# Feature norms in a layer step: the mean by a constant matrix, 1/rms on 352 columns

## The chip, the cores and the metric

The kernel runs on one core of a Trainium2 chip. The metric is the device time of one execution in microseconds (us). A core has five engines that run side by side, each through its own instructions in their order: TensorE (PE in the profile; PEld is its weight load), VectorE (DVE), ScalarE (ACT), GpSimd (POOL) and SyncE (SP). TensorE writes to PSUM, a small memory of banks; VectorE and ScalarE read from it, and GpSimd does not in this kernel. Transfers between memory and the core are started from the queues of SP, POOL and ACT.

## The reference

One encoder layer for 2048 prompt tokens and 64 sample tokens, 1024 features each, in float32. Cut to what matters:

```python
def rms_norm(x, g):
    return x * lax.rsqrt(jnp.mean(x * x, axis=-1, keepdims=True) + EPS) * g

h = rms_norm(x, g_pre)
proj = h @ w_in                       # ten parts: vA, bA, cA, zA, q, f, iv, zB, gA, gB
yA = (silu(zA) * bA * causal_conv3(cA * vA, conv_w)) @ w_a_out
S_new, o = hgrn2_scan(S0, qq, kk, vv, logf)           # eight heads, chunks of 64 tokens
yB = (norm_per_head(o) * g_onorm * silu(zB)) @ w_b_out
out = (sigmoid(gA) * yA + sigmoid(gB) * yB) @ w_o
x = x + rms_norm(out, g_post)                         # first feature norm
gate = sigmoid(rms_norm(x, g_ple) @ w_ple_gate)       # second feature norm
x = x + (p @ w_ple_proj) * gate
```

## The kernel before

**Layout and blocks.** Features lie on the 128 partitions (eight tiles of 128 for 1024 features), tokens along the free axis. The 2112 tokens are cut into three blocks of 704, numbered 0 to 2, and each block into two halves of 352. A matrix product is written as three: the high part of the weights times the high part of the data, high times low, and low times high, each as a matmul on 352 columns in the type float32r. High parts are casts on ACT, low parts subtractions on DVE (`split`, line 184; for weights lines 214 and 184). Large products over weight pairs run as groups of seven smaller ones (`sgroup`, lines 357 to 359, and `in_turn`, lines 490 to 492); plain ones run through `mm3` (lines 523 to 525).

**Order of the work.** Every engine's order is fixed when the program is built. PE's is the leading one: after each product a hook (`hook`) may emit one step of a side job, and `placed` sets that step's matmuls behind the product just issued. Side jobs are Python generators: each `next` emits the work up to the next `yield`.

**The norms.** At the end of a block `final_norm` works as such a side job: first norm, scaling (line 1162), adding of x (1163), squares for the second norm (lines 629, 632, 633), second norm, scaling (1176) and split. In blocks 0 and 1 it runs on both halves together, among the gate groups of the next block, and `spread_out` gives its steps to the hooks in the pattern (0, 1, 0, 1), then (0, 1, 0) eight times, and so on. In block 2 there are two such jobs, one for each half: the first begins among the last products with `w_o` and the second runs in the gate products at the end. The ordering set of `behind_all` puts a step behind the copies and adds that the running products need.

**Inside a norm.** `acc` holds, for each token column, the squares summed over the eight feature tiles, still spread over 128 partitions. `col_rstd` (line 614) takes 128 columns of `acc` at a time as weights and multiplies them with a column of ones: the sum over partitions comes out with tokens on partitions, three columns for 352 tokens. `rstd_of` (line 585 on DVE, line 587 on POOL) computes (mean + EPS) to the power -0.5 on these three columns. `spread` (line 598) multiplies each column, repeated 128 times as weights, with the identity: each token's value stands again in all 128 partitions. Line 624 copies that from PSUM. `rms` does the first part in its first step and the spread and copy in its second.

**Who else calls these.** `rstd_of` also serves the norms of the attention heads (four columns or one) and the rows of x (one column, or six at the start). `spread` also serves the rows of x: at the start, and in `spread_all` for blocks 1 and 2.

**Queues and buffers.** Weights come in on SP's queue. POOL's queue fetches x for the residual (line 1153), spills gates and x (lines 738 and 1172), fetches them back (1043) and writes the output (1197). 52 ring buffers of 708 columns hold most tiles, five PSUM banks the products (`pg`) and three the small ones (`pa`).

Of the kernel before, what the change touches and what calls it, by code (L numbers as in the profile page):

```python
# [10 lines left out]
F32 = mybir.dt.float32  # L11
F32R = mybir.dt.float32r
I32 = mybir.dt.int32
AF = mybir.ActivationFunctionType
ALU = mybir.AluOpType
# [3 lines left out]
P = 128  # L19
D = 1024  # L20
# [62 lines left out]
def hybrid_step(  # L83
# [17 lines left out]
    V, A, G, T, SP = nc.vector, nc.scalar, nc.gpsimd, nc.tensor, nc.sync  # L101
# [3 lines left out]
    const = ctx.enter_context(tc.tile_pool(name="const", bufs=1))  # L105
# [9 lines left out]
    def nm(s):  # L115
        uid[0] += 1
        return f"{s}_{uid[0]}"

    def rt(n=BN, dt=F32):
        t = ring.tile([P, BN + 4], dt, tag="r", name=nm("r"))  # L120
        return t if n is None else t[:, :n]
# [4 lines left out]
    def ps_attn():  # L126
        return psa.tile([P, 512], F32, tag="pa", name=nm("pa"))
# [4 lines left out]
    def spill(kind, j):  # L132
        return dram.tile([P, BN], F32, tag=f"{kind}{j}", name=nm(kind), bufs=2)


    ident = const.tile([P, P], F32, tag="ident", name="ident")
    make_identity(nc, ident)
    ones = const.tile([P, 1], F32, tag="ones", name="ones")
    V.memset(ones, 1.0)
    mhalf = const.tile([P, 1], F32, tag="mhalf", name="mhalf")  # L140
    V.memset(mhalf, -0.5)
    vec = const.tile([P, 9, KB], F32, tag="vec", name="vec")
# [40 lines left out]
    def split(src, hi, lo):  # L183
        return A.copy(hi, src).ins, V.tensor_tensor(lo, src, hi.bitcast(F32), ALU.subtract).ins  # L184
# [49 lines left out]
    last, hooks, copies, adds = [None], [], [None], [None]  # L234

    def placed():

        return tc.issue_after(last[0]) if last[0] is not None else nullcontext()
# [288 lines left out]
    def cols_of(s):  # L527
        return slice(s["off"], s["off"] + s["n"])
# [51 lines left out]
    def tiles_of(n):  # L580

        return [(i, min(i * P, n - P)) for i in range((n + P - 1) // P)]

    def rstd_of(ms_ap, out_ap, scale, start=0):
        scaled = V.tensor_scalar(out_ap, ms_ap, scale, EPS, ALU.mult, ALU.add).ins
        shape = [out_ap.shape[0], out_ap.shape[1]]
        G.tensor_tensor(out_ap, out_ap, mhalf[start : start + shape[0], :].to_broadcast(shape), ALU.pow)
        return scaled

    def cols_tile(n):  # L590
        return small.tile([P, (n + P - 1) // P], F32, tag=f"cols{n}", name=nm("cols"))

    def spread(cols, n):

        pb = ps_attn()
        with placed():
            for i, o in tiles_of(n):
                T.matmul(pb[:, o : o + P], cols[:, i : i + 1].to_broadcast([P, P]), ident, start=True, stop=True)
        return pb[:, :n]

    def spread_all(cols):

        rs = rt()
        for h in range(2):
            A.copy(half(rs, h), spread(cols[h], HN))
        return rs

    def col_rstd(acc, n):

        pc = ps_attn()  # L610
        cols = cols_tile(n)
        with placed():
            for i, o in tiles_of(n):
                T.matmul(pc[:, i : i + 1], acc[:, o : o + P], ones, start=True, stop=True)
        rstd_of(pc[:, : cols.shape[1]], cols, 1.0 / D)
        return cols

    def rms(acc, out, segs, copy=A.copy):


        cols = [col_rstd(acc[:, cols_of(sg)], sg["n"]) for sg in segs]
        yield
        for sg, col in zip(segs, cols):
            copy(out[:, cols_of(sg)], spread(col, sg["n"]))
        yield

    def sum_squares(j, src, acc, n):
        if j == 0:
            A.activation(acc, src, AF.Square)
        else:  # L630
            sq = rt(n)
            A.activation(sq, src, AF.Square)
            V.tensor_tensor(acc, acc, sq, ALU.add)
# [507 lines left out]
    def final_norm(bl, segs, xo, acc, h2, kept):  # L1141


        c = slice(segs[0]["off"], segs[-1]["off"] + HN)
        n = len(segs) * HN
        acc2, rs, rs2 = rt(), rt(), rt()
        xks = []

        def fetch():
            j = len(xks)  # L1150
            if j < KB:
                xks.append(rt())
                G.dma_start(xks[j][:, c], x_fm[j * P : (j + 1) * P, segs[0]["t0"] : segs[0]["t0"] + n])

        for _ in range(2 if bl["last"] else 4):
            fetch()
        copy = V.tensor_copy if bl["last"] else A.copy
        yield from rms(acc, rs, segs, copy)
        for j in range(KB):
            fetch()  # L1160
            xj = xo[j][:, c]
            V.scalar_tensor_tensor(xj, xj, g_post[:, j : j + 1], rs[:, c], ALU.mult, ALU.mult)
            V.tensor_tensor(xj, xj, xks[j][:, c], ALU.add)
            for i in (j - 1,) if 0 < j < KB - 1 else (j - 1, j) if j else ():
                sum_squares(i, xo[i][:, c], acc2[:, c], n)
            yield
        yield from rms(acc2, rs2, segs, copy)
        for j in range(KB):
            xj = xo[j][:, c]
            if kept is not None:  # L1170
                kept["x", j] = spill("x", j)
                G.dma_start(kept["x", j], xo[j])
            if len(h2) <= j:
                h2.append((rt(dt=F32R), rt(dt=F32R)))
            t = rt()
            V.scalar_tensor_tensor(t[:, c], xj, g_ple[:, j : j + 1], rs2[:, c], ALU.mult, ALU.mult)
            split(t[:, c], h2[j][0][:, c], h2[j][1][:, c])
            yield
# [116 lines left out]
    with behind_all(done):  # L1295
        rs = rt()
        cols = [spread(ss[:, 0, 3 * h : 3 * h + 3], HN) for h in range(2)]
        done = A.copy(half(rs, 0), cols[0]).ins, V.tensor_copy(half(rs, 1), cols[1]).ins
# [21 lines left out]
    for bi, bl in enumerate(blocks):  # L1320
        first, kept = bi == 0, kepts[bi]
        segs = bl["segs"]
# [4 lines left out]
        cols, a_first = [], []  # L1327
# [18 lines left out]
        mg, xo, h2, acc = [], [], [], rt()  # L1346
        if first:
            mg = merge(bl, a, kept, sums_ahead)
        else:
            parts = [None] * KB  # L1350

            def made(j, h):

                if nxt:
                    if parts[j] is None:
                        parts[j] = rt(dt=F32R), rt(dt=F32R)
                    split(half(mg[j], h), *(half(t, h) for t in parts[j]))

            stages, loads = merge_in_turn(a, kept, mg, made)
            if not nxt:  # L1360
                stages.append(out_in_turn(mg, xo, acc))
            loads(W_A, -1)
            for idx, n in in_turn(stages, a_first):
                loads(idx, n)
                if (idx, n) == (W_B, 5) and not nxt:
                    ph = [split_rt(raw) for raw in load_p(bl, G)]
                if (idx, n) == (W_O, 4):
                    norms = [final_norm(bl, [s], xo, acc, h2, None) for s in segs]
                    spread_out((norms[0], (1, 0, 1, 1, 1, 1, 1, 1)))
            if nxt:  # L1370
                mg = parts
        if nxt:
            hc = new_operands()
            ops = operands(hc, spread_all(cols), partial(load_x, nxt))
            for j, _ in enumerate(final_out(segs, mg, xo, acc, KB - 1 if first else KH - 1)):
                if j in (1, 3, 5, 7):
                    run(ops, 1)
            fills = gates(nxt, hc, kepts[bi + 1], False)
            norm = final_norm(bl, segs, xo, acc, h2, kept)
            spread_out((norm, (0, 1, 0, 1) + (0, 1, 0) * KB + (1, 0, 1) + (0, 1) * KB))  # L1380
            run(fills, LEAD)
            assert not hooks
            run(final_gate(bl, segs, xo, h2, kept))
        else:
            gate = [final_gate(bl, [s], xo, h2, kept, anew=s is segs[1]) for s in segs]
            spread_out((norms[0], (2, 1, 0, 0, 1, 1, 4, 4)), (norms[1], (0,) * 6 + (1, 1) + (2, 2, 2, 2, 1, 0, 1, 3, 3, 2)))
            run(ple(bl, ph, kept))
            run(gate[0])
            assert not hooks
            run(gate[1])  # L1390
# [49 lines left out]
```

## Time and profile before

| | |
|---|---|
| Median of 3 runs | 2664.5 us (2657.28 to 2667.55) |
| Profiled execution, span | 2661.4 us |
| PE busy | 2623.0 us, 99% of the span, 16748 records |
| DVE busy | 1727.0 us, 65% |
| ACT busy | 1449.6 us, 54% |
| POOL busy | 349.1 us, 13% |

The profile is one execution on the chip. A row of the list in order of time gives the start in us from the span's start, the duration in us, the engine, the line of the kernel, the operation, the tiles (out<-in), the shape and a count, and in brackets how long the engine had been idle and who ended that. A row of the groups gives busy time in us and the mean in ns, then the idle time before the group. A row by stage (two times with a colon) gives for PE, PEld, DVE, ACT and POOL the busy time and, in brackets, the number of instructions, then the granted clock of TensorE as a share of full speed, the share of the DMA engines, and GB/s. Matmuls are pipelined: their own durations overlap, and the distance between two starts is what one costs. A float32 matmul leaves two records, a float32r one leaves one.

### The profile page before, as it was taken

How to read it: one execution, taken by the hardware profiler on the slowest of the kernel's cores; microseconds unless marked ns; L12 is line 12 of the kernel's file. 1: busy time of each engine (PE TensorE's matmuls, PEld its weight loads, DVE VectorE, ACT ScalarE, POOL GpSimd, SP SyncE). 2: the span in 40 equal slices, each digit the busy share in tenths (PEclk: the TensorE clock that was granted, in tenths of full speed). 3: DMA queues.
4: the chain of work that ended last, by engine and by line, in shares of the span. 5: the costliest groups of instructions: out<-in, count | busy, mean ns of one | idle time of the engine just before them, and what ended most of it. 6: DMA issues, size and time to landing. Idle time of an engine off the chain costs nothing.

```text
span 2661.4 us, 47775 instructions
## 1 busy us (share of the span) xinstructions
PE 2623.0 (99%) x16748; PEld 2600.4 (98%) x16748; DVE 1727.0 (65%) x3341; ACT 1449.6 (54%) x2782; POOL 349.1 (13%) x649
## 2 busy tenths in 40 slices
PE   7999999999999999999999999999999999999998
PEld 7999999999999999999999999999999999999988
DVE  7788888998667545466645578443355564447857
ACT  5655655454334544566645565454566654445664
POOL 1000000100432210001112210021000000001011
PEclk9999999999999999999999999999999999999999
DMA  8677777898998988776789988599867678889975
GB/s 304 217 263 269 244 260 271 299 316 288 367 344 285 352 289 275 252 227 221 222 287 357 391 304 306 182 352 307 276 218 222 222 224 263 273 274 319 302 234 168
DMA packets 362097, 735.00 MB, mean 276 GB/s; under 512 B 44064, under 2 KB 48704, under 8 KB 361856
## 3 DMA queue, kind: packets, MB, share of 16 engines
q1 hardware_dynamic: 324864, 588.20, 65.9%
q0 software_dynamic: 36704, 143.70, 14.9%
q8 instruction: 132, 2.16, 0.3%
q14 instruction: 109, 0.89, 0.1%
q10 hardware_dynamic: 288, 0.05, 0.0%
HBM read 525.71 MB, written 206.06 MB: 275 GB/s over the span
## 4 chain that ended last, share of the span: by engine, by line
PE 88%; DMA 4%; issue 3%; DVE 3%; ACT 1%; POOL 1%; SPq 0%; DVEq 0%; ACTq 0%; POOLq 0%
PE pg L357 19%; PE pg L358 19%; PE pg L359 19%; PE pg L523 4%; PE pg L525 4%; PE pg L524 4%; PE pg L491 3%; PE pg L490 3%; PE pg L492 3%; PE pa L957 1%; PE pa L921 1%; PE pa L911 1%; PE pa L959 1%; PE pa L910 1%; DMA low<-s 1%
## 5 line engine op out<-in xcount | busy, mean ns | idle before, releaser
L357 PE MATMUL pg<-r,hi 128*128 128x352 f32 x3304 | 1095.0, 332 | 6.8 <-DVE r L403 2.7
L358 PE MATMUL pg<-r,hi 128*128 128x352 f32 x3304 | 1070.1, 324 | 0.0
L359 PE MATMUL pg<-r,lo 128*128 128x352 f32 x2356 | 763.6, 324 | 0.0
L214 ACT CAST hi<-raw 128x512 fp32r<-128x512 f32 x708 | 435.6, 619 | 573.1 <-PE pg L358 206.5
L357 PEld LDWEIGHTS pg<-r,hi 128*128 128x128 f32 x3304 | 624.3, 189 | 12.6 <-DVE r L865 4.6
L358 PEld LDWEIGHTS pg<-r,hi 128*128 128x128 f32 x3304 | 623.9, 189 | 0.0
L359 PEld LDWEIGHTS pg<-r,lo 128*128 128x128 f32 x2356 | 443.9, 188 | 0.0
L359 PE MATMUL pg<-r,s 128*128 128x352 f32 x948 | 306.9, 324 | 0.0
L523 PE MATMUL pg<-r,hi 128*128 128x352 f32 x896 | 289.4, 325 | 3.1 <-ACT r L1194 2.1
L524 PE MATMUL pg<-r,hi 128*128 128x352 f32 x896 | 289.8, 324 | 0.6 <-DVE r L184 0.6
L525 PE MATMUL pg<-r,lo 128*128 128x352 f32 x756 | 244.6, 324 | 0.4 <-DVE lo L184 0.2
L184 ACT CAST hi<-raw 128x512 fp32r<-128x512 f32 x234 | 143.4, 619 | 165.4 <-PE pg L358 48.3
L184 DVE TENSOR_TENSOR r<-r,r 128x352 fp32r<-128x352 f32 (+3 forms) x274 | 169.9, 638 | 60.7 <-ACT r L184 60.0
L184 DVE TENSOR_TENSOR lo<-raw,hi 128x512 fp32r<-128x512 f32 x234 | 159.6, 688 | 65.8 <-ACT hi L184 54.2
L184 ACT CAST r<-r 128x352 fp32r<-128x352 f32 (+3 forms) x274 | 150.4, 578 | 75.1 <-DVE r L666 18.2
L184 ACT CAST hi<-s 128x512 fp32r<-128x512 f32 x160 | 99.1, 619 | 154.8 <-PE pg L358 132.7
L491 PE MATMUL pg<-r,hi 128*128 128x352 f32 x560 | 181.8, 326 | 0.0
L359 PEld LDWEIGHTS pg<-r,s 128*128 128x128 f32 x948 | 178.9, 189 | 0.1
L490 PE MATMUL pg<-r,hi 128*128 128x352 f32 x560 | 178.4, 326 | 0.1
L523 PEld LDWEIGHTS pg<-r,hi 128*128 128x128 f32 x896 | 168.0, 188 | 5.5 <-ACT r L1194 2.4
L524 PEld LDWEIGHTS pg<-r,hi 128*128 128x128 f32 x896 | 168.6, 188 | 2.0 <-DVE r L184 1.7
L371 ACT COPY hf<-pg 128x352 f32<-128x352 f32 x354 | 156.0, 446 | 6.9 <-PE pg L359 6.3
(358 smaller groups left out, 4096.9 us busy)
## 6 DMA issues: line engine op xcount, KB each, us to landing
raw<-w_blk SPq DMA_DIRECT2D x590, 256.0 KB, 4.0
lo<-low SPq DMA_DIRECT2D x404, 256.0 KB, 3.9
raw<-S SPq DMA_DIRECT2D x392, 256.0 KB, 4.1
low<-lo SPq DMA_DIRECT2D x346, 256.0 KB, 3.8
s<-low SPq DMA_DIRECT2D x304, 256.0 KB, 3.9
S<-s SPq DMA_DIRECT2D x160, 256.0 KB, 3.3
r<-w_blk POOLq DMA_DIRECT2D x48, 256.0 KB, 7.3
S<-r POOLq DMA_DIRECT2D x48, 256.0 KB, 6.1
```

The lines of the kernel that those rows point to most:

```text
L184: return A.copy(hi, src).ins, V.tensor_tensor(lo, src, hi.bitcast(F32), ALU.subtract).ins
L214: A.copy(hi, raw)
L357: add(hi[:, k, :], xhi, start=start and k == 0, stop=False)
L358: add(hi[:, k, :], xlo, start=False, stop=False)
L359: last[0] = add(lo[:, k, :], xhi, start=False, stop=k == KH - 1).ins
L371: copied = A.copy(got[n], ps[bank])
L490: add(hi[:, k, :], xhi, start=start and k == 0, stop=False)
L491: add(hi[:, k, :], xlo, start=False, stop=False)
L492: last[0] = add(lo[:, k, :], xhi, start=False, stop=k == KH - 1).ins
L523: T.matmul(ps, hi[:, k % 4, :], xhi[:, c], start=k == ks[0], stop=False)
L524: T.matmul(ps, hi[:, k % 4, :], xlo[:, c], start=False, stop=False)
L525: last[0] = T.matmul(ps, lo[:, k % 4, :], xhi[:, c], start=False, stop=k == ks[-1]).ins
```

## The change

`col_rstd` goes, and `rms` no longer turns tokens onto partitions. Its first step splits the squares `acc` into a high and a low part. Its second step multiplies both with a constant 128x128 matrix that holds 1/1024 everywhere: the mean over all features comes out in all 128 partitions for 352 columns. `rstd_of` then works on these 352 columns, DVE reading them from PSUM and POOL taking the power, straight into the tile that the scaling reads; copies from PSUM fall away. The constant is built by one DVE operation from the identity in place of the column of ones. In `spread`, which remains for the rows of x, the product with the identity becomes a transposition.

```diff
-    ones = const.tile([P, 1], F32, tag="ones", name="ones")
-    V.memset(ones, 1.0)
+    mean = const.tile([P, P], F32R, tag="mean", name="mean")
+    V.tensor_scalar(mean, ident, 0.0, 1.0 / D, ALU.mult, ALU.add)
...
-                T.matmul(pb[:, o : o + P], cols[:, i : i + 1].to_broadcast([P, P]), ident, start=True, stop=True)
+                T.transpose(pb[:, o : o + P], cols[:, i : i + 1].to_broadcast([P, P]), ident)
...
-    def col_rstd(acc, n):
-
-        pc = ps_attn()
-        cols = cols_tile(n)
-        with placed():
-            for i, o in tiles_of(n):
-                T.matmul(pc[:, i : i + 1], acc[:, o : o + P], ones, start=True, stop=True)
-        rstd_of(pc[:, : cols.shape[1]], cols, 1.0 / D)
-        return cols
-
-    def rms(acc, out, segs, copy=A.copy):
-
-
-        cols = [col_rstd(acc[:, cols_of(sg)], sg["n"]) for sg in segs]
+    def rms(acc, out, segs):
+
+
+        hi, lo = rt(dt=F32R), rt(dt=F32R)
+        for sg in segs:
+            c = cols_of(sg)
+            split(acc[:, c], hi[:, c], lo[:, c])
         yield
-        for sg, col in zip(segs, cols):
-            copy(out[:, cols_of(sg)], spread(col, sg["n"]))
+        for sg in segs:
+            c, ps = cols_of(sg), ps_attn()[:, : sg["n"]]
+            with placed():
+                T.matmul(ps, mean, hi[:, c], start=True, stop=False)
+                T.matmul(ps, mean, lo[:, c], start=False, stop=True)
+            rstd_of(ps, out[:, c], 1.0)
         yield
...
-        copy = V.tensor_copy if bl["last"] else A.copy
-        yield from rms(acc, rs, segs, copy)
+        yield from rms(acc, rs, segs)
...
-        yield from rms(acc2, rs2, segs, copy)
+        yield from rms(acc2, rs2, segs)
```

## The prediction

> **What bounds the kernel.** I read the page first (busy times, groups), then the groups of POOL with shapes kept apart, then the lists in order of time around the places where the feature norms are computed, engine by engine, and last who waited for whom on PE.
>
> ```profile
> span 2661.4 us, 47775 instructions
> PE 2623.0 (99%) x16748; PEld 2600.4 (98%) x16748; DVE 1727.0 (65%) x3341; ACT 1449.6 (54%) x2782; POOL 349.1 (13%) x649
> ```
>
> PE is in use for 99% of the span; POOL for 13%. So what the change takes from PE is worth its full length, and what it adds to POOL, ACT or DVE costs nothing unless PE must wait for it. The question is therefore how long the new power takes, and how soon somebody needs it.
>
> **The power, c.** It is computed at line 587 by POOL. Today it runs on 1, 3, 4 or 6 columns of 128 partitions.
>
> ```profile
> L587 POOL TENSOR_TENSOR ms<-ms,mhalf 128x4 f32<-128x4 f32 x24 | 26.1, 1088 | 223.6 <-DVE ms L585 223.6
> L587 POOL TENSOR_TENSOR ms<-ms,mhalf 128x1 f32<-128x1 f32 x24 | 13.3, 554 | 100.2 <-DVE ms L585 100.2
> L587 POOL TENSOR_TENSOR cols<-cols,mhalf 128x3 f32<-128x3 f32 x12 | 11.1, 926 | 92.8 <-DVE cols L585 92.8
> L587 POOL TENSOR_TENSOR rows<-rows,mhalf 128x6 f32<-128x6 f32 x1 | 1.4, 1412 | 0.0
> masks.py:199 POOL TENSOR_SCALAR_AFFINE_SELECT ident<-ident x1: 304/304/304, 2.2 to 2.2; 128x128 f32<-128x128 f32 x1
> ```
>
> The four sizes take 554, 926, 1088 and 1412 ns. Each column more costs 186 ns (1 to 3), 162 (3 to 4) and 162 (4 to 6); the least-squares line is 396 + 171 n ns. At n = 352 it gives 60.7 us. The flattest pair, carried on from the six columns, gives 1.412 + 346 x 0.162 = 57.5 us, the steepest 65.8 us. The other end is the one row with a wide tile on this engine: 128 columns of a select in 0.304 us, so 352 in 0.84 us. I take 60.7, because those rows are of this very operation and grow almost in a straight line with no sign of a fixed charge shared by several columns. The extrapolation, by a factor of 59, is the weakest step here.
>
> The Trainium skill (GPSIMD Engine Reference, section 3.1) puts a two-input elementwise operation of this engine at about 2.6 cycles of 1.2 GHz an element: an estimate of 352 x 2.6 / 1.2 = 0.76 us for such a row. That page speaks of an add; it gives no figure for a power. By that rule the whole change would come out as the first rival below; the trace's slope, 171 ns a column, is some 80 times the rule's 2.2 ns.
>
> **What PE gains.** Per half of 352 tokens and norm, three 128x1 products (L614) and three 128x128 (L598) become two of 128x352.
>
> ```profile
> 879.03 1.47 PE L614 MATMUL pa<-ones,r 128*128 128x1 f32 x12
> 880.36 0.41 PE L359 MATMUL pg<-r,lo 128*128 128x352 f32 x1
> 880.61 0.32 PE L357 MATMUL pg<-r,hi 128*128 128x352 f32 x1
> ...
> 882.88 0.32 PE L359 MATMUL pg<-r,s 128*128 128x352 f32 x1
> 883.04 1.50 PE L598 MATMUL pa<-ident,cols 128*128 128x128 f32 x12
> 884.30 0.41 PE L357 MATMUL pg<-r,hi 128*128 128x352 f32 x1
> ```
>
> Two halves: L614 holds PE 1.33 us (879.03 to 880.36), L598 1.26 us; 14 wide products take 2.27 us, 0.162 each, so the four new ones take 0.65. Gain 1.94 a pair, six pairs: 12 us. An f32 product leaves two records (x12 for six), a transposition one, so the 18 spreads that remain (12 for x's rows in blocks 1 and 2, 6 at the start) save about 18 x 0.11 = 2 us.
>
> **Where the power is needed.** In the built order the split comes at the norm's first step, the products, L585 and the power at its second, two matrix products of PE later, and the scaling that reads the result at the third. Before, the power had four such steps. DVE works in its order, so when L1162 or L1176 waits, all that DVE does for the running products (L377, L382, L403) waits behind it, ACT's squares and casts behind those, and PE when its banks and weights run out. POOL's own queue waits too: spills (L738, L1172) and fetches (L1153) stand behind the powers.
>
> *First norm, blocks 0 and 1, two powers in a row:*
>
> ```profile
> 877.01 1.88 DVE L633 TENSOR_TENSOR r<-r,r 128x704 f32<-128x704 f32 x2
> ...
> 885.19 1.81 DVE L1162 SCALAR_TENSOR_TENSOR r<-r,vec,r 128x704 f32<-128x704 f32 x2 [2.51 <-ACT r L624]
> ```
>
> ```profile
> 888.87 0.63 ACT L214 CAST hi<-raw 128x512 fp32r<-128x512 f32 x1
> ```
>
> ```profile
> 895.98 0.32 PE L357 MATMUL pg<-r,hi 128*128 128x352 f32 x1
> ```
>
> The sum is ready at 878.9. The new products stand 14 matmuls behind L614's old place, 881.1; with 0.3 for them and 0.5 for L585 the first power starts near 882.2, and with one DMA issue between them (about 0.5) both end at 882.7 + 2c. From L1162 to the end of the weight cast behind ACT's square took 4.3 us (885.19 to 889.50); that cast now stands behind the square and is the first one of the next group, which PE began at 895.98. So PE gets there at 887.0 + 2c: later by 2c - 9.0, gains on PE before it included.
>
> *Second norm, blocks 0 and 1:*
>
> ```profile
> 926.54 1.47 PE L614 MATMUL pa<-ones,r 128*128 128x1 f32 x12 [1.44 <-DVE r L633]
> ```
>
> ```profile
> 927.88:931.36 3.48, 3.48 (x14) 3.48 (x14) 0.16 (x1) 0.01 (x1) 1.46 (x2) 0.53 1.04 407
> ```
>
> ```profile
> 937.27 0.94 DVE L1176 SCALAR_TENSOR_TENSOR r<-r,vec,r 128x704 f32<-128x704 f32 x1
> ...
> 941.15 0.51 DVE L403 TENSOR_TENSOR r<-hf,pg 128x352 f32<-128x352 f32 x1
> ```
>
> ```profile
> 946.30 0.32 PE L357 MATMUL pg<-r,hi 128*128 128x352 f32 x1
> ```
>
> PE waits 1.44 us for the squares here and then runs 3.48 us at a granted clock of 0.53 (14 matmuls instead of 21, 1.2 us lost). The split takes that wait off PE. Free at 925.1, it does two products (24 x 0.162 = 3.9), then the four new ones: power from about 930.2, both ended at 930.2 + 2c. L1176 to the end of the L403 that frees a bank took 4.4 us; PE needs that bank at 946.30. So 934.6 + 2c against 946.3: 2c - 11.7. I use the same for block 1.
>
> *Block 2, one half at a time, four single powers:*
>
> ```profile
> 2557.13 0.52 DVE L403 TENSOR_TENSOR r<-r 128x352 f32<-128x352 f32 x1
> ...
> 2559.74 0.52 DVE L624 COPY r<-pa 128x352 f32<-128x352 f32 x1
> ...
> 2560.60 1.08 DVE L1162 SCALAR_TENSOR_TENSOR r<-r,vec,r 128x352 f32<-128x352 f32 x2
> ...
> 2583.40 0.59 DVE L1176 SCALAR_TENSOR_TENSOR r<-r,vec,r 128x352 f32<-128x352 f32 x1
> ...
> 2600.23 1.08 DVE L1162 SCALAR_TENSOR_TENSOR r<-r,vec,r 128x352 f32<-128x352 f32 x2
> ...
> 2617.72 0.58 DVE L1176 SCALAR_TENSOR_TENSOR r<-r,vec,r 128x352 f32<-128x352 f32 x1
> ```
>
> ```profile
> 2581.97 0.83 PE L598 MATMUL pa<-ident,cols 128*128 128x128 f32 x6
> ```
>
> ```profile
> 2611.37 0.43 PE L523 MATMUL pg<-r,hi 128*128 128x352 f32 x1 [2.07 <-ACT r L1194]
> ```
>
> ```profile
> 2614.23 1.59 POOL L587 TENSOR_TENSOR cols<-cols,mhalf 128x3 f32<-128x3 f32 x1
> ```
>
> Here DVE and ACT lead and PE follows, so I compare DVE's own instructions. L585 now makes 352 columns out of PSUM, as L624 did (0.52). First: L585 stands before the L403 of 2557.13, the scaling goes at 2557.2 + c instead of 2560.60: c - 3.4. Second: products where L598 stood (2581.97), power from 2582.5, against 2583.40: c - 0.9. Third: L585 now stands behind all scalings of the first half, where L624 stood just before 2600.23, so its power no longer runs ahead beside them: c + 0.1; PE has no reserve, it waited 2.07 us there already. Fourth: power from about 2614.8, against 2617.72: c - 2.9, and some 2 us more of PE's first-half products as cover: c - 5. Sum: 4c - 9.2.
>
> **What else.** The split (ACT cast and DVE subtraction of 352 columns, both at most 0.53 us) is in the starts above. The constant is one DVE operation on 128x128 at the start in place of a memset, under 0.52 us, set against the spread there; a few casts at the start and weight loads change places: 0, bounds -1 and +1. Two more ring tiles a norm: 0, since the sum shows nobody short of them for the two steps that they live. After each of eight long waits PE restarts at the low clock (1.2 us each by the row above, up to twice that) and DVE has less lead (about 1 us): +18.
>
> **Sum.** Blocks 0 and 1: 2 x (2c - 9.0) + 2 x (2c - 11.7) = 8c - 41.4. Block 2: 4c - 9.2. Restarts +18, spreads -2. Together 12c - 35 = 728 - 35 = +693 us. On the profiled execution's 2661.4 that is 3354; the median of the runs, 2664.5, lies 3.1 above it: 3358. With c from 57.5 to 65.8: 3320 to 3420, and 10 more for the covers: 3310 to 3430.
>
> **Rivals.**
> *A wide power is cheap (faster).* If POOL works through a long row at the pace of its select (c = 0.84), the waits fit in the covers above: 2c = 1.7 against 9.0 and 11.7. Then only gains stay: 8 us of products in blocks 0 and 1, 2 of spreads, twice the wait and slow clock (2 x 2.7), some 2 in block 2: about 18 us, 2646. It decides below c = 4.5, where 2c equals the first cover. For it: a wide row exists at that pace. Against: three steps of the same slope. Chance 0.10.
>
> *A long row is cheaper per column than a short one (slower, by less).* Say half the slope: c = 30, 12 x 30 - 35 = +325, 2990. For it: the row's loop is seen to six columns only. Against: the last two steps are no flatter than each other. Chance 0.15, spread from 2700 to 3300.
>
> *Nothing to be measured.* c near 4, covers used up and no more: within 13 us of before. Chance 0.03. That the change doesn't take effect is excluded: the built order has the twelve wide powers and no L614.
>
> *Straight line, my forecast:* 0.72. Within it, POOL's spills and fetches behind the powers may add some us a site; that is in the upper end.
>
> The range, 2980 to 3440, holds the straight line and half of the cheaper-row case. Half a per cent, 13 us, is about what a measurement of this kernel can tell from none. Faster 0.10, same 0.03, slower 0.87.
>
> **What would show it.** Groups: L587's wide form x12 at about 61 us each, POOL busy near 349 + 12 x 60 = 1070 us. Lists in order of time: in blocks 0 and 1 PE idle about 110 us at four places, DVE's L1162 or L1176 with a wait of some 120 us on POOL; in block 2 four of about 60. Slices of the span: holes in PE there and nowhere else. It would be wrong if a wide power takes a few us, or if PE goes on through them because other work than I listed is free to run.

## The result, and the profile after

The changed kernel takes 3303.4 us (median; 3299.6 to 3309.4) where the kernel before takes 2664.6 us (2657.3 to 2667.6) beside it: 1.240 times as long, with a 95% interval of 1.237 to 1.242. The profiled execution has a span of 3302.0 us, 640.6 more than before. The prediction was 3358 us, with a range of 2980 to 3440. One run of the experiment with the transpositions alone, further down, took 3428.6 us at a granted clock of 0.70, and its median leaves that run out.

The page of the changed kernel: the span, the busy times, three rows of the 40 slices (tenths of busy time for PE and POOL, tenths of full clock for PEclk), the chain that ended last, and three of the costliest groups (busy us, mean ns of one, then the idle time before them and who ended it). Line numbers moved a little: the scalings are now 1158 and 1172.

```profile
span 3302.0 us, 47520 instructions
...
PE 2628.0 (80%) x16610; PEld 2602.5 (79%) x16610; DVE 1735.7 (53%) x3349; ACT 1452.3 (44%) x2786; POOL 1018.2 (31%) x649
...
PE   8999999999805099999999970519999999992314
...
POOL 1000011044396910011221049681000000107885
PEclk9999999999957599999999985759999999996666
...
PE 65%; POOL 15%; issue 13%; DMA 3%; DVE 3%; ACT 1%; SPq 0%; POOLq 0%; DVEq 0%; ACTq 0%
...
L587 POOL TENSOR_TENSOR r<-r,mhalf 128x352 f32<-128x352 f32 x12 | 677.6, 56473 | 116.3 <-DVE r L585 116.2
...
L1158 DVE SCALAR_TENSOR_TENSOR r<-r,vec,r 128x704 f32<-128x704 f32 (+1 forms) x32 | 23.9, 765 | 337.6 <-POOL r L587 337.6
L1172 DVE SCALAR_TENSOR_TENSOR r<-r,vec,r 128x704 f32<-128x704 f32 (+1 forms) x32 | 24.2, 763 | 331.9 <-POOL r L587 331.9
```

PE works as long as before (2628.0 us against 2623.0), but in 80% of the span and not in 99%. The missing time lies in three holes of its row: two where blocks 0 and 1 end, one in the last four slices. In the same slices POOL's row fills up. The twelve wide powers take 56.47 us each, 677.6 in all; DVE's scalings waited 337.6 + 331.9 = 669.5 us for them, somewhat more than the 640.6 us by which the span grew.

One site in order of time (changed kernel; start, duration, engine, line, and in brackets the idle time before and who ended it), from the squares of block 0's first norm to PE's restart, and then PE's other restarts in block 0 and in block 2:

```profile
879.28 1.88 DVE L630 TENSOR_TENSOR r<-r,r 128x704 f32<-128x704 f32 x2
...
883.98 1.01 DVE L585 TENSOR_SCALAR r<-pa 128x352 f32<-128x352 f32 x2
...
884.59 56.47 POOL L587 TENSOR_TENSOR r<-r,mhalf 128x352 f32<-128x352 f32 x1 [20.00 <-DVE r L585]
941.65 56.46 POOL L587 TENSOR_TENSOR r<-r,mhalf 128x352 f32<-128x352 f32 x1
...
998.14 1.81 DVE L1158 SCALAR_TENSOR_TENSOR r<-r,vec,r 128x704 f32<-128x704 f32 x2 [112.29 <-POOL r L587]
...
1002.15 0.66 PE L357 MATMUL pg<-r,hi 128*128 128x352 f32 x1 [105.96 <-ACT hi L214]
1154.49 0.66 PE L357 MATMUL pg<-r,hi 128*128 128x352 f32 x1 [103.86 <-ACT hi L214]
...
3034.72 0.66 PE L491 MATMUL pg<-r,hi 128*128 128x352 f32 x1 [56.03 <-DVE r L184]
3113.58 0.66 PE L523 MATMUL pg<-r,hi 128*128 128x352 f32 x1 [54.48 <-ACT r L184]
3196.03 0.66 PE L523 MATMUL pg<-r,hi 128*128 128x352 f32 x1 [58.80 <-ACT r L1190]
3260.11 0.66 PE L523 MATMUL pg<-r,hi 128*128 128x352 f32 x1 [49.36 <-ACT hi L184]
```

Two powers in a row end at 998.11, the scaling goes at once, and PE follows 4.0 us later, when ACT's weight cast behind the square is done. Block 1 repeats the first two waits (106.02 and 103.88 us). The eight waits of PE add up to 638.4 us.

What follows on a wait, by stage (changed kernel; PE, PEld, DVE, ACT, POOL busy with counts, then granted clock, share of the DMA engines, GB/s):

```profile
898.00:1002.00 104.00, 0.00 (x0) 0.00 (x0) 3.86 (x6) 1.21 (x2) 102.42 (x8) 0.52 0.04 12
1002.15:1006.00 3.85, 3.85 (x13) 3.85 (x14) 3.85 (x6) 2.02 (x4) 1.33 (x3) 0.50 0.96 335
1006.00:1008.00 2.00, 2.00 (x12) 2.00 (x11) 1.86 (x4) 0.54 (x1) 1.07 (x2) 0.76 0.95 346
1154.49:1160.00 5.51, 5.51 (x19) 5.51 (x20) 4.26 (x7) 4.66 (x9) 1.14 (x2) 0.50 0.75 260
```

During the wait nothing else is left to do: DVE, ACT and the DMA stand still as well. Then PE runs at half clock until about 1007.0 (the 0.76 is the mean of a half and a full part): 16 products in 4.8 us where full speed, at 0.162 us each, has 30. This restart costs some 2.2 us. Behind the second norm's wait (last row) the half clock lasts longer still, until about 1160.6.

### The profile page after: what moved, and what is told of

Read it like the earlier page. It is cut to its first block, busy times and chain, and to the rows that moved or that the text cites. A ratio compares the mean times of both kernels' runs of the same rounds, so it can differ in the third digit from the quotient of the medians.

```text
span 3302.0 us, 47520 instructions
## 1 busy us (share of the span) xinstructions
PE 2628.0 (80%) x16610; PEld 2602.5 (79%) x16610; DVE 1735.7 (53%) x3349; ACT 1452.3 (44%) x2786; POOL 1018.2 (31%) x649
## 4 chain that ended last, share of the span: by engine, by line
PE 65%; POOL 15%; issue 13%; DMA 3%; DVE 3%; ACT 1%; SPq 0%; POOLq 0%; DVEq 0%; ACTq 0%
PE pg L357 15%; PE pg L359 15%; PE pg L358 15%; POOL r L587 14%; PE pg L491 3%; PE pg L490 3%; PE pg L492 3%; PE pg L523 2%; PE pg L524 2%; PE pg L525 2%; PE pa L954 1%; PE pa L918 1%; PE pa L908 1%; PE pa L956 1%; DMA low<-s 1%
## 5 line engine op out<-in xcount | busy, mean ns | idle before, releaser
L357 PEld LDWEIGHTS pg<-r,hi 128*128 128x128 f32 x3304 | 626.0, 189 | 433.5 <-ACT hi L214 422.9
L587 POOL TENSOR_TENSOR r<-r,mhalf 128x352 f32<-128x352 f32 x12 | 677.6, 56473 | 116.3 <-DVE r L585 116.2
L358 PEld LDWEIGHTS pg<-r,hi 128*128 128x128 f32 x3304 | 626.4, 190 | 0.0
L523 PEld LDWEIGHTS pg<-r,hi 128*128 128x128 f32 x896 | 170.8, 191 | 166.7 <-ACT r L1190 59.1
L1158 DVE SCALAR_TENSOR_TENSOR r<-r,vec,r 128x704 f32<-128x704 f32 (+1 forms) x32 | 23.9, 765 | 337.6 <-POOL r L587 337.6
L1172 DVE SCALAR_TENSOR_TENSOR r<-r,vec,r 128x704 f32<-128x704 f32 (+1 forms) x32 | 24.2, 763 | 331.9 <-POOL r L587 331.9
```

Source lines behind the costliest of these rows:

```text
L357: add(hi[:, k, :], xhi, start=start and k == 0, stop=False)
L358: add(hi[:, k, :], xlo, start=False, stop=False)
L523: T.matmul(ps, hi[:, k % 4, :], xhi[:, c], start=k == ks[0], stop=False)
```

## Experiments

The theory (A) was the prediction's, with the measured size: twelve powers of 56.5 us, each longer than its cover, and nothing else of weight. The rivals put a part of the time on what else came with the change: the split and products in a new place, the steps of lead that the power lost, the PSUM read that moved to DVE, or a price that does not go by columns.

### The same work with a multiplication for the power

```diff
-    def rstd_of(ms_ap, out_ap, scale, start=0):
+    def rstd_of(ms_ap, out_ap, scale, start=0, op=ALU.pow):
...
-        G.tensor_tensor(out_ap, out_ap, mhalf[start : start + shape[0], :].to_broadcast(shape), ALU.pow)
+        G.tensor_tensor(out_ap, out_ap, mhalf[start : start + shape[0], :].to_broadcast(shape), op)
...
-            rstd_of(ps, out[:, c], 1.0)
+            rstd_of(ps, out[:, c], 1.0, op=ALU.mult)
```

> The changed kernel with a multiplication in place of the power on the 352 columns, on the same engine, tiles and places (so the norms come out wrong: 1/rms is left out). Theory A, the power's own price: the row of line 587 for 352 columns falls from 56.47 us to about 1 us, its waits fit in the covers of 9 to 12 us, and the time is that of the first rival, about 2646 us (2638 to 2656), under the kernel before. Theory B, the two steps of lead that the power lost and the added split make the waits: the time stays above 3200. Theory C, any two-input operation of POOL on a wide row with a repeated second input is slow: the row stays near 56 us and the time near 3303.

Measured: 2651.0 us, 0.996 times the kernel before (0.994 to 0.997); span 2646.2. The busy times, line 587 and those who waited for it, and one row of PE:

```profile
PE 2603.7 (98%) x16610; PEld 2580.3 (98%) x16610; DVE 1736.0 (66%) x3349; ACT 1449.9 (55%) x2786; POOL 347.6 (13%) x649
```

```profile
L587 POOL TENSOR_TENSOR r<-r,mhalf x12: 768/778/1049, 881.6 to 2601.8; 128x352 f32<-128x352 f32 x12
...
  DVE r L1158: 3.4, 4
  DVE r L1172: 1.0, 1
```

```profile
902.62 0.43 PE L359 MATMUL pg<-r,s 128*128 128x352 f32 x1 [1.37 <-DMA s<-low]
```

The order, the queues, the split, the products and what each engine has to wait for are those of the changed kernel; one operation differs, and the whole loss is gone. The wide operation takes 0.78 us (shortest, middle, longest: 768, 778, 1049 ns), and the scalings wait 4.4 us for it in all in place of 669.5. This also measures what the rest of the change is worth: PE's busy time falls by 19.3 us, the span by 15.2, the median by 13.8. It is the kernel that the first rival had in mind, with 2651 against its 2646. The Trainium skill (GPSIMD Engine Reference, section 3.1), which led to an estimate of 0.76 us for a row of 352, comes near the 0.778 us of the multiplication in its total (its slope is looked at under the sizes below). The power of the same shape takes 73 times as long.

A part of the gain is lost again where the DMA is full. The products of PE come in the same order in all these kernels, so the start of each, set against its start in the kernel before, gives the lead at that point. By that count this kernel is 2.9 us ahead at 900 us and 1.3 at 905 (times of the kernel before). The row above stands between: PE waits 1.37 us for a low part that is still under way, and the kernel before has no such wait there.

### Power on half of the columns

```diff
-            rstd_of(ps, out[:, c], 1.0)
+            q = sg["n"] // 2
+            rstd_of(ps[:, :q], out[:, c][:, :q], 1.0)
+            rstd_of(ps[:, q:], out[:, c][:, q:], 1.0, op=ALU.mult)
```

(`op` is the argument added above.)

> The changed kernel with the power on the first 176 columns of each half and a multiplication on the other 176 (so half of the norms are wrong). Theory A, a price by columns, 0.159 us each from the rows 128x4 (1.04) and 128x352 (56.47): about 28.4 us for the power and 0.9 for the rest, so by 12 x price - 37 a time near 2664.5 + 315 = 2979. Rival: a price by instruction (loading code, a handshake for each): near 3303, and the row near 56 us.

Measured: 2970.7 us, 8 us under the expectation, a ratio of 1.115 (1.113 to 1.118); span 2967.6. POOL's group, with power and multiplication mixed, and two of PE's waits:

```profile
L587 POOL TENSOR_TENSOR r<-r,mhalf 128x176 f32<-128x176 f32 x24 | 347.1, 14471 | 114.2 <-DVE r L585 91.8 <-ACT r L1026 20.0 <-ACT r L1192 2.2
```

```profile
944.79 0.66 PE L357 MATMUL pg<-r,hi 128*128 128x352 f32 x1 [50.64 <-ACT hi L214]
2784.01 0.66 PE L491 MATMUL pg<-r,hi 128*128 128x352 f32 x1 [28.52 <-DVE r L184]
```

347.1 us over twelve pairs is 28.9 a pair: half the columns, half the price. PE's waits halve with it, from 105.96 to 50.64 and from 56.03 to 28.52. The time goes by the columns that the power is taken of.

### The price, size by size

A copy of the kernel before, with powers and multiplications of several widths behind its last work on POOL:

```diff
+    src, dst = rt(), rt()
+    V.memset(src, 2.0)
+    for op in (ALU.pow, ALU.mult):
+        for n in (8, 16, 32, 64, 128, 256, 352):
+            G.tensor_tensor(dst[:, :n], src[:, :n], mhalf.to_broadcast([P, n]), op)
+    for p in (16, 64):
+        G.tensor_tensor(dst[:p, :128], src[:p, :128], mhalf[:p].to_broadcast([p, 128]), ALU.pow)
```

> The kernel before with scratch operations of POOL after its last transfers, of which nothing is used: powers on 8, 16, 32, 64, 128, 256 and 352 columns, multiplications on the same, and powers on 128 columns of 16 and of 64 partitions. Straight line: powers at 0.4 + 0.159 n us (1.7, 2.9, 5.5, 10.6, 20.8, 41.1, 56.4), and 16 partitions as slow as 128. If a row of more than six columns is handled in another way, a step between 4 and 8 or later and a flatter line behind it. Multiplications: near 2.6 cycles of 1.2 GHz a column if the Trainium skill (GPSIMD Engine Reference, section 3.1) has it right, 0.76 us and a fixed part for 352.

The one run took 2845.3 us with this work added. Groups of POOL in that stretch: three of the powers and two of the multiplications at line 1397, then the powers on fewer partitions at line 1400:

```profile
L1397 POOL TENSOR_TENSOR r<-r,mhalf 128x352 f32<-128x352 f32 x1 | 56.4, 56415 | 0.1
L1397 POOL TENSOR_TENSOR r<-r,mhalf 128x256 f32<-128x256 f32 x1 | 41.1, 41115 | 0.1
L1397 POOL TENSOR_TENSOR r<-r,mhalf 128x128 f32<-128x128 f32 x1 | 20.7, 20725 | 0.1
...
L1397 POOL TENSOR_TENSOR r<-r,mhalf 128x352 f32<-128x352 f32 x1 | 0.8, 772 | 0.1
...
L1397 POOL TENSOR_TENSOR r<-r,mhalf 128x128 f32<-128x128 f32 x1 | 0.4, 398 | 0.1
...
L1400 POOL TENSOR_TENSOR r<-r,mhalf 64x128 f32<-64x128 f32 x1 | 20.7, 20708 | 0.1
L1400 POOL TENSOR_TENSOR r<-r,mhalf 16x128 f32<-16x128 f32 x1 | 20.7, 20705 | 0.1
```

The power is a straight line to the end: from 128 to 256 columns 20.4 us more, from 256 to 352 15.3, which is 159 ns a column both times. And it does not matter how many partitions hold a value: 16, 64 and 128 partitions pay the same 20.7 us for 128 columns. So a spread value costs no more than another one in its column, but 352 columns cost 352 columns. The multiplication grows by 1.67 ns a column ((772 - 398) / 224), less than the 2.2 ns of the expectation; with a fixed part of about 0.2 us it comes to the 0.77 all the same.

### Products and power one step earlier

```diff
             split(acc[:, c], hi[:, c], lo[:, c])
-        yield
         for sg in segs:
...
             rstd_of(ps, out[:, c], 1.0)
         yield
+        yield
```

> The changed kernel with the products, L585 and the power moved into the norm's first step, beside the split; the second step is empty. The power starts two matrix products (3.9 us) earlier less the 1.5 us or so for which it now waits for the split. Theory A, a wait is worth the power less its lead: 8 places x 2.4 to 3.9 us less, 3303 - 19 to 31 = 3272 to 3284. Rival, the lead doesn't count because the engines refill what they lost: 3303 within 6 us.

Measured: 3299.1 us, a ratio of 1.239: 4 us less than the changed kernel where 19 to 31 were expected. Theory A missed; the rival's 3303 within 6 us holds. The power's start and PE's waits:

```profile
884.09 56.47 POOL L587 TENSOR_TENSOR r<-r,mhalf 128x352 f32<-128x352 f32 x1 [20.00 <-DVE r L585]
...
1001.64 0.66 PE L357 MATMUL pg<-r,hi 128*128 128x352 f32 x1 [105.96 <-ACT hi L214]
1036.98 0.43 PE L618 MATMUL pa<-r,mean 128*128 128x352 f32 x1 [1.68 <-ACT r L184]
1153.83 0.66 PE L357 MATMUL pg<-r,hi 128*128 128x352 f32 x1 [101.87 <-ACT hi L214]
```

At the first site the sum of the squares was ready at 880.66 and the power began 3.43 us later; in the changed kernel it was 881.16 and the same 3.43 us. What lies between is the split, the products and line 585, and the second step stood so close that nothing waited for it. At the second norm the split is waited for instead (1.68 us at line 618), and the wait after it is 2 us shorter. The change takes one of the power's two steps of lead away, and this run gives it back: it was worth some 4 us over all sites, of the 640.

### The new norms in block 2 alone

```diff
-        yield from rms(acc, rs, segs)
+        wide = bl["last"] is True
+        yield from rms(acc, rs, segs) if wide else rms_cols(acc, rs, segs, V.tensor_copy if bl["last"] else A.copy)
```

(`rms_cols` is the `rms` of before, and the second norm has the same edit.)

> The changed norms in block 2 alone, the old ones in blocks 0 and 1; transpositions as in the changed kernel. By the four long waits of PE in block 2 of the changed kernel's trace (56.0, 54.5, 58.8, 49.4, together 218.7 us): 2664 + 219 = 2883, 2870 to 2890. If the waits in block 2 and in the others fed on one another (a queue of spills that is left over, say), it would come out well below that.

Measured: 2886.3 us, a ratio of 1.084 (1.082 to 1.086); span 2882.4, which is 221.0 more than before. PE's waits:

```profile
2616.03 0.66 PE L493 MATMUL pg<-r,hi 128*128 128x352 f32 x1 [56.00 <-DVE r L186]
...
2695.74 0.66 PE L525 MATMUL pg<-r,hi 128*128 128x352 f32 x1 [54.51 <-ACT r L186]
2777.26 0.66 PE L525 MATMUL pg<-r,hi 128*128 128x352 f32 x1 [58.80 <-ACT r L1212]
2841.01 0.66 PE L525 MATMUL pg<-r,hi 128*128 128x352 f32 x1 [49.70 <-ACT hi L186]
```

They are the four of the changed kernel to within 0.4 us. The sites add up: block 2 gives 221, and the 420 that remain are what PE waited at the four places in blocks 0 and 1 of the changed kernel (419.7). That block 2 does not hide waits of the other blocks is what lets the prediction add them.

### The transpositions alone

```diff
-                T.matmul(pb[:, o : o + P], cols[:, i : i + 1].to_broadcast([P, P]), ident, start=True, stop=True)
+                T.transpose(pb[:, o : o + P], cols[:, i : i + 1].to_broadcast([P, P]), ident)
```

(in the kernel before, so all 54 spreads change, not only the 18 that the change keeps)

> The kernel before with the transposition in place of the product with the identity, everywhere in the spreads (54 of them), and nothing else of the change. By one record of about 0.11 us less for each: 6 us less, 2658.5 (2655 to 2662), which is at the limit of what can be told from no change. If a transposition of f32 takes two records as the product does: no difference.

Measured: 2663.9 against 2664.4 us, a ratio of 0.9996 (0.9988 to 1.0005): nothing, where a gain of some us was expected. The expectation missed. The spreads in this kernel (all but the six at the start), its PE row behind the first site, and a stretch of it:

```profile
L598 PE MATMUL pa<-ident,cols 128*128 128x128 f32 x48 | 7.1, 279 | 0.0
```

```profile
902.41 0.43 PE L359 MATMUL pg<-r,s 128*128 128x352 f32 x1 [1.86 <-DMA s<-low]
```

```profile
900.00:920.00 20.00, 18.14 (x113) 17.85 (x112) 12.93 (x20) 12.13 (x23) 3.23 (x6) 1.00 1.03 383
```

The same stretch of the kernel before:

```profile
900.00:920.00 20.00, 20.00 (x126) 20.00 (x126) 12.73 (x19) 10.68 (x21) 2.69 (x5) 1.00 1.03 400
```

The spreads did get cheaper: one record in place of two, and a pair of halves 0.68 us shorter on PE. By the count of products this kernel is 4.0 us ahead of the one before at 900 us and 1.5 at 905; between them stands the wait of 1.86 us for a low part, which the kernel before does not have. In block 1 it goes the same way, from 3.0 us to 0.2. The DMA engines are full in that stretch in both kernels (1.03, with 383 and 400 GB/s), so it is likely that a lead there only means waiting for a transfer. It is not shown: no run has less traffic there.

Two things speak for care. The kernel with the powers of several sizes runs the same program as the kernel before until 2650 us, and its one execution wandered between 1.0 us behind and 3.5 us ahead of it, so most of the 4.0 us may be no gain of the transpositions at all. And a kernel with no lead loses time in that stretch too, as the last experiment shows.

### Another way to 1/rms: a root on ACT, a reciprocal on DVE

```diff
+    eps = const.tile([P, 1], F32, tag="eps", name="eps")
+    V.memset(eps, EPS)
...
-            rstd_of(ps, out[:, c], 1.0)
+            A.activation(out[:, c], ps, AF.Sqrt, bias=eps, scale=1.0)
+            V.reciprocal(out[:, c], out[:, c])
```

> The changed kernel with the power done elsewhere: ACT takes the square root of mean + EPS from PSUM, DVE the reciprocal; POOL has no part in the feature norms. Theory A: like the multiplication, about 2646, plus some of the twelve added table loads of ACT (1.28 us each), 4 to 8 us where ACT leads in block 2: 2650 to 2658, a little under the kernel before. Theory B (lost lead and added split make the waits): above 3200.

Measured: 2661.4 us, a ratio of 0.9990 (0.9981 to 0.9998), 3 us above the upper end expected. ACT's table loads (the kernel before has one at its line 725, none at the other two), and two of PE's waits (us in total, times, longest):

```profile
L623 ACT ACT_TABLE_LOAD x6 | 7.7, 1283 | 1.7 <-PE pa L622 1.7
L725 ACT ACT_TABLE_LOAD x5 | 6.4, 1283 | 0.1
L1193 ACT ACT_TABLE_LOAD x2 | 2.6, 1283 | 0.0
```

```profile
PE pg L525 <- ACT r L1193: 5.9, 1, 5.9
PE pg L361 <- DMA lo<-low: 5.6, 3, 2.8
```

The first of these waits in the kernel with the multiplication, which has no root and none of the added loads:

```profile
PE pg L523 <- ACT r L1190: 5.3, 1, 5.3
```

The root takes 0.56 us and needs no POOL, but going from it to the sigmoids and back costs a table load of 1.283 us each time, twelve more in all. One might put the long wait of PE in block 2 down to them: 5.9 us for the sigmoid behind such a load, where the kernel before waited 2.07. But the kernel with the multiplication waits 5.3 us at the same place without a load, so that wait belongs to the new norms and not to the root. The Trainium skill (ScalarE: Activation LUTs, section "What ACT_TABLE_LOAD costs") puts a switch at 2.66 us, of which 1.38 are a drain beside the load. The load agrees, the drain does not show here: in the next experiment a load stands from 883.76 to 885.04 and the root starts at 885.06.

### The same, with block 2 as before

```diff
+        wide = bl["last"] is False
+        yield from rms(acc, rs, segs) if wide else rms_cols(acc, rs, segs, V.tensor_copy if bl["last"] else A.copy)
```

> Blocks 0 and 1 take the new norms with ACT's square root and DVE's reciprocal in the place of the power; block 2 keeps the norms of the kernel before. With ACT's square root in all blocks the work was 2.7 us ahead of the kernel before when block 0's and 1's norms were done, and that lead was gone at the end of block 2, where nothing was gained even without any price for the power. If the sites add up, the end is 2.7 us earlier than before and a little more, since the spreads of block 2 are transpositions here: a span of 2658 (2654 to 2661), a ratio of about 0.998. If the loss at the end had another cause than block 2's own norms (the last sigmoids, say), the time is that of the kernel before, within 1 us.

Measured: 2653.4 against 2663.6 us, a ratio of 0.9955 (0.9941 to 0.9968). The span is 2653.4 us. The busy times, and ACT's table loads (one of those at line 746 is in the kernel before as well):

```profile
PE 2612.9 (98%) x16638; PEld 2590.1 (98%) x16638; DVE 1747.0 (66%) x3351; ACT 1463.7 (55%) x2798; POOL 342.0 (13%) x641
```

```profile
L746 ACT ACT_TABLE_LOAD x5 | 6.4, 1283 | 0.1
L625 ACT ACT_TABLE_LOAD x4 | 5.1, 1283 | 0.1
```

This is the fastest kernel of the study with the whole computation: about 10 us, 0.45%, less than the one before. It came out 4.6 us below the span expected. By the count of products the lead ahead of block 2's norms was 8.7 us here and 4.5 with the root everywhere (the expectation had put the latter at 2.7), though the norms of blocks 0 and 1 are written alike. Where the two part is the DMA-bound stretch of block 0: from 900 to 916 us this kernel goes from 0.5 us behind the kernel before to 2.6 behind, with a wait of 1.77 us for a low part; the one with the root everywhere goes from 0.7 ahead to 6.0 behind, with one of 2.78. Why, was not followed further; it is not the lead, which this kernel did not have. Block 2 then gives back 0.7 us here, 4.9 with the root everywhere, and 1.1 with the multiplication. So the root in block 2 was a cost of some 4 us there; how much of it is the four table loads, and how much the rest of the work put on ACT and DVE, is not separated.

## Why the prediction was right, and where it was off

**The mechanism** was right at each point: a wide power that outlasts its cover, PE waiting at four places of two powers and four of one, POOL busy 1018 us (1070 predicted), the waits of DVE 110 to 112 us at the four double sites (some 120 predicted, with the larger c). The multiplication in its place takes all of it away, half the columns take half, and block 2 alone gives its share.

**The size of c** is where the 55 us to the prediction lie. The step took the least-squares line through 1, 3, 4 and 6 columns, 171 ns a column, and so 60.7 us; measured were 56.47, below even the lower bound of 57.5. Between 128 and 352 columns a column costs 159 ns, much as between 3 and 6 columns (162). What pulled the line up is the step from one column to three (186 a column). Twelve times 60.7 - 56.47 is 51 us. With the measured c the prediction's own sum, 12c - 35, gives 642.7; measured were 640.6. The flattest of the three pairs, taken from the widest rows, would have been the better line for a far extrapolation.

**The terms -35** came out right nearly one by one. Counted by PE's products, the lateness of the changed kernel behind a wait and its restart, less the lateness ahead of the site, is what the site cost:

| Site | predicted, with c = 56.47 | measured |
|---|---|---|
| first norm, blocks 0 and 1 | 2c - 9.0 + 2.2 = 106.1 each | 106.2, 106.2 |
| second norm, blocks 0 and 1 | 2c - 11.7 + 2.2 = 103.4 each | 101.6, 99.8 |
| block 2 | 4c - 9.2 + 8.8 = 225.5 | 224.1 |
| elsewhere | -2 | 2.7 |

At the first norms the sum was right to 0.1 us. The changed kernel was 2.3 us late there already, before any of the new norms had run (the squares stand at 879.28 against 877.01). That is no more than two executions of one program can part, as the kernel with the powers of several sizes shows. Less these 2.3 us the power began at 882.3, where 882.2 was predicted.

At the second norms the power began as predicted too (at 1039.27; less the 109.4 us by which the kernel was late there, that is 929.9, and 930.2 was predicted). But PE followed 2.4 us behind the end of the two powers (1152.1 to 1154.5) and not 4.4: it waited for ACT's cast at line 214, as its row says, and not for the bank that line 403 frees. That step of the sum was 2 us too long. In block 1 this execution of the kernel before also loses more at that place, which the change wins back: its clock stands at 0.52 for 6.8 us there, and at 0.54 for 3.4 us in block 0. The sum had used block 0 for both.

**Restarts.** After the four double waits the half clock lasted 4.8, 6.1, 4.6 and 5.8 us and cost 2.0 to 2.7 us each, at the upper end of the 1.2 to 2.4 that the sum used; after three of the four single ones it lasted 3.2 to 6.2 us, after the last 9.9 with other waits between. The Trainium skill (TensorE: Matmul & The Clock Gate, Part 1) has a free-running window of 3.4 us that must be busy before the clock is whole again. All of these times but the last lie between about one and two such windows.

**What PE gains.** As work of PE the gains stand: 19.3 us less busy in the kernel with the multiplication. That what is taken from PE is worth its full length, as the prediction has it, is too strong. The spreads alone changed the time by nothing that could be measured. And of the 18.2 us by which the kernel with the multiplication is ahead at 2600 us, 3.3 go at its next wait for the last sigmoids (5.3 us against 2.07), which is much of why the first rival's 2646 came out as 2651.

**The steps of lead.** The prediction gives the power four such steps before. By the steps of the norm it is two from the power to the scaling (four matrix products of PE) before, and one after. The loss of one is no term of the sum, since the sum counts the cover from the start of the power. Given back, it was worth 4 us, so leaving it out was no large error.

**The rivals.** A cheap wide power was excluded by one row of the trace after; a cheaper price per column by the row of sizes. That a change of operation alone turns the time of the forecast into that of the first rival shows how much hung on whether the small rows or the wide row stand for a wide power.

## What to carry to other kernels

Before an operation is widened, look for its own rows, not for another operation's of the same shape: here the multiplication of 352 columns takes 0.78 us and the power 56.5, and the four short powers in the trace already had the slope. Carry the line on from the widest rows, and set the result against the time to the first one who needs it, site by site; POOL's 13% of busy time said nothing about that. And a gain on the bounding engine is only as good as what comes next: here a part of it was lost again at waits for transfers and for the last sigmoids.

## What the runs showed of the hardware

- POOL's power costs about 0.4 us and 159 ns a column ((56.47 - 0.4) / 352), whether 16, 64 or 128 partitions hold values; a multiplication costs 0.40 us for 128 columns and 0.77 for 352.
- A spread as a transposition leaves one record where the float32 product with the identity leaves two, and takes 0.68 us less for six of 128x128.
- After PE's waits of 54 to 106 us its granted clock was 0.50 for 3.2 to 6.2 us (seven waits; the four double ones cost 2.0 to 2.7 us each).
- In a stretch with the DMA at a share of 1.03, a lead of 4.0 us on PE became 1.5 at a wait for a transfer.
- A table load on ACT took 1.283 us and was followed by its function after 0.02 us.
